# A two-block sequence model on one core: side sequences moved inside a merge of generators, two scheduling offsets exchanged, weight pieces cut in halves

## Chip, cores, metric

The kernel runs on one core of one Trainium2 chip, as one launch. The metric is the device time of that launch in microseconds; the median of several runs is compared.

## What is computed

Two blocks on 256 tokens of width 2048, in float32. The first block has two layers over a latent sequence x and a context of 256 tokens; the second block is a single layer with four mixers, cross attention and a gated feed-forward. The change touches layer 0 (`even_mixer`) and layer 1 (`odd_mixer`) of the first block:

```python
def wkv7_scan(state, inputs, reverse):
    def step(S, xs):
        r, w, k, v, a, b = xs
        sa = jnp.einsum('bhvk,bhk->bhv', S, a)
        S = S * w[:, :, None, :] + sa[..., None] * b[:, :, None, :] + v[..., None] * k[:, :, None, :]
        return S, jnp.einsum('bhvk,bhk->bhv', S, r)
...
def even_mixer(hl, hc, w_in, w_out, ...):
    al, rl, kl, vl, wdl, adl, gl = split_even(hl @ w_in)
    ac, rc, kc, vc, wdc, adc, gc = split_even(hc @ w_in)
    for d, reverse in enumerate((False, True)):
        in_c = rwkv_dir_inputs(rc, kc, vc, wdc[..., d, :], adc[..., d, :], *dir_p, reverse)
        in_l = rwkv_dir_inputs(rl, kl, vl, wdl[..., d, :], adl[..., d, :], *dir_p, reverse)
        s_ctx, y_c = wkv7_scan(s0, in_c, reverse)
        _, y_l = wkv7_scan(s_ctx, in_l, reverse)
        outs_l.append(rwkv_readout(y_l, in_l, r_k, gn_g[d], gn_b[d]))
...
def odd_mixer(hl, hc, w_in, w_out, q_g, k_g, cos, sin, need_ctx_out):
    ql, kl, vl, gl = jnp.split(hl @ w_in, ...)
    ol = blocked_attention(ql, k_all, v_all)
    yl = (ol.reshape(B, T, ATT_W) * jax.nn.silu(gl)) @ w_out
```

## The kernel before

**Numbers.** A float32 product of a large weight is made of fast passes: a weight piece is loaded as `raw`, cast to `whi` on ACT and its rest `raw - whi` put into `wlo` on DVE (`wsplit`, L187 and L188), and PE multiplies both halves. A piece is 128 partitions x 1024 columns in most of the kernel. `wsplit` cuts it into `s.nsplit` parts along its first free axis; `s.nsplit` is 1, and 2 inside `l0` (`small_stream`, L499 and L500, has pieces of 128x512 of its own there).

**Layer 0's recurrence.** It is done in chunks of 64 tokens. There are 16 units: 8 pairs of heads times 2 directions, 8 chunks each (4 of context, then 4 of x). A unit goes through generators, each of which emits some instructions per step and yields:

- `wkv_prep`, the preparation: shifts of r, k, v, two LoRA products (L625, L626), the decay scan (L638), the sum of squares of the keys (L641), the bonus (L671), the scaled keys BK (L680, L682). 14 steps.
- `wkv_inv`, the inverse: the stacked operand S (L704, L705) and BH (L710), then eight products per group of four chunks (L725), emptied by three DVE operations per half (L726, L730, L731), then the inverse of a triangular 64x64 block per chunk and head by products in the "iv" buffers (L741), each followed by DVE (L748 to L771). 20 steps.
- `wkv_rows`: transposes into "sc" buffers (L781, L789) and ACT copies out of them (L784, L786, L790), for four chunks at a time.
- `wkv_chain`, the serial part: per chunk the products L809, L815, L819 and the outputs L823, L824; between them R on DVE (L811), UV on ACT (L816) and the next state ZV on DVE (L822). 24 steps.
- `wkv_read`, the read-out: a mean (L841), a variance (L848, L849), an inverse root (L851) and the result (L853 to L856). 6 steps.

**The PSUM buffers.** There are eight banks: "acc", "sc" and "iv" have two buffers each, "ch" and "yb" one. Rows, the first products of the inverse, the preparation and the read-out all take "sc" in turn.

**The order.** `l0_body` runs a software pipeline: in turn n it merges the chain of unit n, the inverse of unit n+1, and, as side sequences, the read-out of unit n-1 and the preparation of unit n+2. `merge(a, b, side)` is a loop: in each pass it advances the inverse a by 3/4 of a step (by one, where there is no chain), the chain b by one, and each side sequence by one, and then emits `fill`, an even share of the dense products of layer 0 that are still open (L509 to L511) and of the modulation products (L369, L382, L392). A turn has some 26 passes. PE's order is exactly the order in which the code emits (`manual_schedule(engines={ET.PE})`). DVE, ACT, POOL and SP are ordered by a list scheduler at build time: among instructions that it takes to be ready, the one with the lowest number goes first; the number is the place in the program, less an offset given by `s.prio(n)`, which calls `high_priority(offset=n)`:

```python
    def prio(s, n):
        return s.tc.high_priority(offset=n) if n else contextlib.nullcontext()
```

On the chip every engine works through its own list in that order.

**Layer 1** (`l1`) gets its 140 weight pieces through `stream`, which splits a piece ahead of its use; layer 0's output projection (`l0_out_n`) is emitted in `l1` for three of its four column blocks, 24 more pieces.

Of the kernel before, what the change touches and what calls it, by code (L numbers as in the profile page):

```python
# [136 lines left out]
class _K:  # L137
# [729 lines left out]
    def l0_body(s):  # L867
# [60 lines left out]
        def fill(t):  # L928
            nonlocal F
            credit[0] += t  # L930
            while credit[0] > 0.0:
                c = next(F, None)
                if c is None:
                    return
                credit[0] -= c
                left[0] -= c
# [7 lines left out]
        def prep(n):  # L944
            p, d = units[n]
            if d == 0:
                while s.have_rkv < p:
                    fill(0.6)
                s.raw = s.l0_raw(p)
                s.outp = s.T("op", [P, 512], bufs=3)  # L950
            u = _U(p, d, s.raw, s.outp)
            u.h = [None, None]
            return u, s.wkv_prep(u)
# [2 lines left out]

        def merge(a, b, side):

            due = 0.25
            while a is not None or b is not None:  # L960
                due += 0.75 if b is not None else 1.0
                if a is not None and due >= 1.0:
                    due -= 1.0
                    with s.prio(100):
                        if next(a, None) is None:
                            a = None
                if b is not None:
                    with s.prio(60):
                        if next(b, s) is s:
                            b = None  # L970
                for x in side:
                    next(x, None)
                steps[0] = max(steps[0] - 1.0, 1.0)
                fill(left[0] / steps[0])
            for x in side:
                for _ in x:
                    pass

# [5 lines left out]
        cur, pg = prep(0)  # L984
# [12 lines left out]
        F = filler([r.rearrange("p (k c) -> p k c", k=2) for r in raw[0:2]])  # L997
        credit[0], left[0] = 0.0, 29 * 16 * 0.64 + 16 * (4 * 0.6 + 0.9)
        nxt, pg = prep(1)
        merge(s.wkv_inv(cur, 1), None, [pg])  # L1000
        s.wkv_rows(cur, 0)
        rg = []
        for n in range(16):
            s.wkv_rows(cur, 1)
            nx2, pg = prep(n + 2) if n < 14 else (None, iter(()))
            if n == 15:
                for _ in F:
                    pass
                s.out0 = F = s.l0_out_n(0)
                credit[0], left[0], steps[0] = 0.0, 26, 24.0  # L1010
            merge(s.wkv_inv(nxt, n % 2) if nxt else None, s.wkv_chain(cur, nxt, rg), rg + [pg])
            rg = [s.wkv_read(cur)]
            cur, nxt = nxt, nx2
        for _ in rg[0]:
# [1115 lines left out]
def build(tc, I, O, dbg=False, upto=99):  # L2130
    nc = tc.nc
    s = _K(tc, I, O, dbg)
    s.nraw = 4
    s.nhi = 2
    s.nsplit = 1
    s.ivn = [0, 0]
    s.psb = {"acc": 2, "sc": 2, "iv": 2, "ch": 1, "yb": 1}
    with tc.tile_pool(name="sb", bufs=1) as s.pool, tc.tile_pool(name="ps", bufs=1, space=PSUM) as s.psum, \
            tc.tile_pool(name="dr", bufs=1, space=DRAM) as s.dpool:
        ET = mybir.EngineType  # L2140
        head = s.head()
        with tc.manual_schedule(engines={ET.PE, ET.Activation}):
            next(head)
        with tc.manual_schedule(engines={ET.PE}):
            next(head, None)
            s.l0()
            s.mem_again()
            s.l1()
        s.block2()


# [16 lines left out]
```

## Time and profile before

| | |
|---|---|
| median of 3 runs | 3675.69 us (3669.39 to 3677.23) |
| the profiled execution | 3661.04 us |
| its span, first to last instruction | 3659.3 us |
| PE busy | 3455.7 us, 94% |
| weight loads of PE busy | 2701.6 us, 74% |
| DVE busy | 2189.3 us, 60% |
| ACT busy | 1637.9 us, 45% |
| mean granted clock of PE | 0.978 |

Busy time is the union of an engine's instructions over the span. The granted clock is a share of TensorE's full 2.4 GHz. A wait is idle time of an engine ahead of an instruction, put down to the instruction that released it last. The recurrence lies at about 590 to 1600 us, layer 1 at about 1790 to 2290 us.

### The profile page before, as it was taken

What the parts mean: (1) busy time and instruction counts of PE and PEld (TensorE: products, weight loads), DVE (VectorE), ACT (ScalarE), POOL (GpSimd) and SP (SyncE); (2) the same over time, 40 slices, a digit from 0 to 9 for tenths busy, and PEclk for the clock granted to TensorE, in tenths of its full rate; (3) what the DMA queues carried; (4) which work ended last, traced back from release to release, by engine and by line L of the source; (5) the groups of instructions that cost most, each with busy time, mean ns of one, the idle gap of its engine ahead of it and who ended that gap; (6) DMA issues with size and microseconds to landing.
All of it is one profiled execution on the core that took longest, in us unless ns stands there. A gap on an engine that the chain in (4) does not pass through costs nothing.

```text
span 3659.3 us, 56514 instructions
## 1 busy us (share of the span) xinstructions
PE 3455.7 (94%) x22385; PEld 2701.6 (74%) x22385; DVE 2189.3 (60%) x3813; ACT 1637.9 (45%) x2661; POOL 67.4 (2%) x136
## 2 busy tenths in 40 slices
PE   6999999989988888899999999998999999999998
PEld 3577775666666666678788888777888888888886
DVE  4254456667667666753656667766654566666544
ACT  3254224444454444431445555454454544444433
POOL 1000000000000000000000000000000000000000
PEclk9999999999999999999999999998999999999999
DMA  9974434433334333443434457553665566666654
GB/s 312 316 254 122 128 108 152 134 106 119 120 110 129 106 109 118 153 125 110 131 111 142 127 170 210 153 138 100 184 179 163 182 190 190 190 190 190 201 190 162
DMA packets 656579, 578.58 MB, mean 158 GB/s; under 512 B 25819, under 2 KB 499343, under 8 KB 656314
## 3 DMA queue, kind: packets, MB, share of 16 engines
q1 hardware_dynamic: 627936, 538.86, 49.0%
q10 hardware_dynamic: 24474, 29.09, 2.4%
q0 software_dynamic: 3904, 7.01, 0.7%
q8 instruction: 176, 2.88, 0.3%
q14 instruction: 89, 0.73, 0.1%
HBM read 547.32 MB, written 27.56 MB: 157 GB/s over the span
## 4 chain that ended last, share of the span: by engine, by line
issue 59%; PE 27%; DVE 5%; ACT 3%; DMA 2%; POOL 0%; ACTq 0%; SPq 0%; DVEq 0%; POOLq 0%
PE acc L509 4%; PE acc L510 4%; PE acc L511 4%; PE iv L741 3%; PE acc L369 2%; PE ch L815 1%; PE acc L207 1%; PE ch L819 1%; DMA sgT<-ev 1%; PE ch L809 1%; PE sc L725 1%; PE yb L823 1%; PE yb L824 0%; PE acc L1627 0%; PE acc L1628 0%
## 5 line engine op out<-in xcount | busy, mean ns | idle before, releaser
L188 DVE TENSOR_TENSOR wlo<-raw,whi 128x1024 fp32r<-128x1024 f32 (+2 forms) x742 | 850.9, 1150 | 850.6 <-ACT whi L187 845.5
L187 ACT CAST whi<-raw 128x1024 fp32r<-128x1024 f32 (+2 forms) x742 | 732.2, 990 | 1060.0 <-PE acc L207 209.7
L207 PE MATMUL acc<-A,whi 128*128 128x512 f32 x1488 | 530.1, 397 | 2.6 <-DVE A L1059 1.5
L208 PE MATMUL acc<-A,wlo 128*128 128x256 f32 x1488 | 423.3, 285 | 0.9 <-DVE wlo L188 0.9
L509 PE MATMUL acc<-A,whi 128*128 128x512 f32 x768 | 353.0, 460 | 18.5 <-ACT ev L520 12.4
L207 PEld LDWEIGHTS acc<-A,whi 128*128 128x128 f32 x1488 | 277.9, 187 | 66.8 <-DVE A L1059 1.8
L510 PE MATMUL acc<-B,whi 128*128 128x512 f32 x768 | 308.5, 402 | 0.0
L511 PE MATMUL acc<-A,wlo 128*128 128x512 f32 x768 | 306.8, 399 | 0.0
L208 PEld LDWEIGHTS acc<-A,wlo 128*128 128x128 f32 x1488 | 280.3, 188 | 5.3 <-DVE wlo L188 2.1
L207 PE MATMUL iv<-A,whi 128*128 128x512 f32 x736 | 257.4, 391 | 0.0
L509 PEld LDWEIGHTS acc<-A,whi 128*128 128x128 f32 x768 | 149.4, 195 | 84.7 <-issue 35.8
L208 PE MATMUL iv<-A,wlo 128*128 128x256 f32 x736 | 206.3, 280 | 2.5 <-DVE wlo L188 2.5
L511 PEld LDWEIGHTS acc<-A,wlo 128*128 128x128 f32 x768 | 148.2, 193 | 34.2
L510 PEld LDWEIGHTS acc<-B,whi 128*128 128x128 f32 x768 | 149.3, 194 | 29.9 <-issue 11.3
L207 PEld LDWEIGHTS iv<-A,whi 128*128 128x128 f32 x736 | 137.7, 187 | 30.3
L208 PEld LDWEIGHTS iv<-A,wlo 128*128 128x128 f32 x736 | 139.1, 189 | 3.1 <-DVE wlo L188 3.1
L500 DVE TENSOR_TENSOR wlo<-raw,whi 128x512 fp32r<-128x512 f32 x116 | 80.0, 689 | 70.1 <-ACT whi L499 69.1
L499 ACT CAST whi<-raw 128x512 fp32r<-128x512 f32 x116 | 71.6, 617 | 112.2 <-PE acc L510 105.3
L816 ACT COPY UV<-ch 64x128 f32<-64x128 f32 x128 | 32.9, 257 | 162.2 <-PE ch L815 152.7
L822 DVE SCALAR_TENSOR_TENSOR ZV<-ZV,We,ch 64x64 f32<-64x64 f32 x224 | 62.0, 277 | 35.4 <-PE ch L819 33.0
L224 PE MATMUL acc<-whi,B 128*128 128x512 f32 x192 | 76.7, 401 | 0.0
L225 PE MATMUL acc<-wlo,B 128*128 128x512 f32 x192 | 75.8, 395 | 0.2 <-DVE wlo L188 0.2
(1577 smaller groups left out, 7076.5 us busy)
## 6 DMA issues: line engine op xcount, KB each, us to landing
raw<-w_gate_up SPq DMA_DIRECT2D x176, 512.0 KB, 4.8
raw<-mod_w SPq DMA_DIRECT2D x128, 512.0 KB, 4.8
raw<-w_down SPq DMA_DIRECT2D x88, 512.0 KB, 4.8
raw<-od_w_in SPq DMA_DIRECT2D x80, 512.0 KB, 3.7
raw<-w_in SPq DMA_DIRECT2D x80, 512.0 KB, 3.9
raw<-w_xkv SPq DMA_DIRECT2D x64, 512.0 KB, 6.5
A<-mod_w SPq DMA_DIRECT2D x64, 512.0 KB, 5.8
raw<-ev_w_in SPq DMA_DIRECT2D x116, 256.0 KB, 3.0
```

The costliest lines, as they stand in the source:

```text
L187: nc.scalar.copy(hi[:, q], raw[:, q])
L188: nc.vector.tensor_sub(lo[:, q], raw[:, q], hi[:, q].bitcast(F32))
L207: s.nc.tensor.matmul(acc, hi, x.rearrange("p a t -> p (a t)"), start=start, stop=False)
L208: s.nc.tensor.matmul(acc[:, 0:256], lo, x[:, 0], start=False, stop=stop)
L224: nc.tensor.matmul(acc, xh, hi[:, kk], start=k == 0, stop=False)
L225: nc.tensor.matmul(acc, xh, lo[:, kk], start=False, stop=False)
L369: nc.tensor.matmul(acc[32 * q:32 * q + 32], s.SC[:, 2 * k:2 * k + 32], pair[q // 2][:, q % 2], start=k < 4, stop=k >= 12, tile_position=(0 ...
L500: nc.vector.tensor_sub(lo, raws[j % 2], hi.bitcast(F32))
L509: s.nc.tensor.matmul(acc, hi[:, k], hX[kx], start=kx == 0, stop=False)
L510: s.nc.tensor.matmul(acc, hi[:, k], lX[kx], start=False, stop=False)
L511: s.nc.tensor.matmul(acc, lo[:, k], hX[kx], start=False, stop=kx == 15)
L741: nc.tensor.matmul(ps[hs[h], c], l(hs[h], c), r(hs[h], c), start=True, stop=True)
```

## The change

In `merge` the inverse is emitted under offset 60 instead of 100 and the chain under 120 instead of 60. A side sequence now comes with the number of the pass from which it is advanced: the read-out from pass 3, the preparation from pass 7, or from pass 5 in the first merge, which has no chain. Before, both were advanced from pass 1. What is left of them at the end of a merge is emitted there, as before. And `l1` runs with `s.nsplit = 2`.

```diff
         def merge(a, b, side):
 
-            due = 0.25
+            due, n = 0.25, 0
             while a is not None or b is not None:
                 due += 0.75 if b is not None else 1.0
                 if a is not None and due >= 1.0:
                     due -= 1.0
-                    with s.prio(100):
+                    with s.prio(60):
                         if next(a, None) is None:
                             a = None
                 if b is not None:
-                    with s.prio(60):
+                    with s.prio(120):
                         if next(b, s) is s:
                             b = None
-                for x in side:
-                    next(x, None)
+                n += 1
+                for x, first in side:
+                    if n >= first:
+                        next(x, None)
                 steps[0] = max(steps[0] - 1.0, 1.0)
                 fill(left[0] / steps[0])
-            for x in side:
+            for x, _ in side:
                 for _ in x:
                     pass
...
-        merge(s.wkv_inv(cur, 1), None, [pg])
+        merge(s.wkv_inv(cur, 1), None, [(pg, 5)])
...
-            merge(s.wkv_inv(nxt, n % 2) if nxt else None, s.wkv_chain(cur, nxt, rg), rg + [pg])
+            merge(s.wkv_inv(nxt, n % 2) if nxt else None, s.wkv_chain(cur, nxt, rg), [(x, 3) for x in rg] + [(pg, 7)])
...
+            s.nsplit = 2
             s.l1()
+            s.nsplit = 1
```

The lines of the generators keep their numbers. The instructions of layer 0 are the same in number and kind on every engine. The list of PE in the opening of one unit, that of the timeline from 997 us, before; L725 are the inverse's products, L848 the read-out's second, L625 and L626 the preparation's LoRA products, L509 to L511 filler, the L8xx of "ch" and "yb" the chain:

```order
L725 MATMUL sc<-S_9494,BK 128x128 x8
L819 MATMUL ch<-UV_9075,BT_9077 128x128
L823 MATMUL yb<-whi,ZV_9076 128x128
L824 MATMUL yb<-pu,UV_9075 128x128
L848 MATMUL sc<-sq,k_65 128x512
L509 MATMUL acc<-A_1576,whi 128x512
L510 MATMUL acc<-B_1584,whi 128x512
L511 MATMUL acc<-A_1576,wlo 128x512
L725 MATMUL sc<-S_9501,BK 128x128 x8
L809 MATMUL ch<-ZV_9076,whi 128x128
L625 MATMUL sc<-TW,m_9531 128x512
L626 MATMUL sc<-TW,m_9531 128x512
```

The same place on PE now; the read-out's first product L841 stands where the second stood, and the second follows L815:

```order
L725 MATMUL sc<-S_9491,BK 128x128 x8
L819 MATMUL ch<-UV_9043,BT_9045 128x128
L823 MATMUL yb<-whi,ZV_9044 128x128
L824 MATMUL yb<-pu,UV_9043 128x128
L841 MATMUL sc<-YS,k_65 128x512
...
L725 MATMUL sc<-S_9498,BK 128x128 x8
L809 MATMUL ch<-ZV_9044,whi 128x128
L509 MATMUL acc<-A_1576,whi 128x512
L510 MATMUL acc<-B_1584,whi 128x512
L511 MATMUL acc<-A_1576,wlo 128x512
L815 MATMUL ch<-R_9578,pw 128x128
L848 MATMUL sc<-sq,k_65 128x512
```

The LoRA products have left the opening. The second place on PE is the middle of a unit, behind the rows of the next one (L781, L789); now L641, the preparation's sum of squares, stands there, as L841 stood behind the rows at a unit's start before:

```order
L781 MATMUL sc<-k_65,m_8831 128x128 x2
L789 MATMUL sc<-k_65,BH 128x128 x4
L809 MATMUL ch<-ZV_9461,wlo 128x128
L641 MATMUL sc<-tb,k_65 128x512
L509 MATMUL acc<-A_1574,whi 128x512
```

Before, L641 stood ahead of these rows, behind the fourth chunk's L809. DVE in the opening of that unit before, up to the chain's second R (L811) and one more; L726, L730 and L731 empty the inverse's products, L853 and L856 are the read-out's last:

```order
L731 TENSOR_TENSOR AB_9510<-sc,k_65 128x4x64
L822 SCALAR_TENSOR_TENSOR ZV_9076<-ZV_9076,We,ch 64x64 x2
L853 TENSOR_TENSOR YS<-YS,sq 128x512
L726 TENSOR_TENSOR raw<-sc,k_65 64x256
L730 TENSOR_TENSOR S_9501<-sc,k_65 64x4x64
L731 TENSOR_TENSOR AB_9513<-sc,k_65 128x4x64
L726 TENSOR_TENSOR raw<-sc,k_65 64x256
L730 TENSOR_TENSOR S_9501<-sc,k_65 64x4x64
L731 TENSOR_TENSOR AB_9513<-sc,k_65 128x4x64
L732 TENSOR_TENSOR raw<-raw,id_83 128x512
L811 TENSOR_TENSOR R_9605<-ch,k_65 128x128
L856 TENSOR_TENSOR op<-op,YS 128x512
```

And DVE there now:

```order
L726 TENSOR_TENSOR raw<-sc,k_65 64x256
L822 SCALAR_TENSOR_TENSOR ZV_9044<-ZV_9044,We,ch 64x64 x2
L731 TENSOR_TENSOR AB_9507<-sc,k_65 128x4x64
L730 TENSOR_TENSOR S_9491<-sc,k_65 64x4x64
L731 TENSOR_TENSOR AB_9507<-sc,k_65 128x4x64
L446 SCALAR_TENSOR_TENSOR vs<-v_9486,PM,tb 128x512
L842 SCALAR_TENSOR_TENSOR YS<-sc,YS 128x512
L726 TENSOR_TENSOR raw<-sc,k_65 64x256
L730 TENSOR_TENSOR S_9498<-sc,k_65 64x4x64
L731 TENSOR_TENSOR AB_9510<-sc,k_65 128x4x64
L811 TENSOR_TENSOR R_9578<-ch,k_65 128x128
L726 TENSOR_TENSOR raw<-sc,k_65 64x256
```

The chain's ZV (L822) and R (L811) moved in between the operations that empty the inverse's products, and L853 moved behind all of them.

## Rows read from the trace of the kernel before

**Rows 1.** Windows by stage: window and length, busy us per engine (instructions), PEclk, DMA, GB/s.

```profile
590.00:1600.00 1010.00, 891.76 (x9390) 636.67 (x9389) 685.93 (x1475) 465.19 (x899) 41.54 (x83) 0.95 0.39 120
...
1790.00:2290.00 500.00, 495.22 (x2383) 402.89 (x2382) 323.86 (x540) 266.77 (x408) 0.00 (x0) 1.00 0.52 154
```

**Rows 2.** Waits of PE, 590 to 1600 us: waiter, awaited, us, times, longest.

```profile
PE sc L625 <- DVE pv L731: 20.8, 14, 3.1
PE sc L625 <- DVE AB L731: 18.2, 12, 2.7
PE sc L841 <- ACT ZV L786: 17.5, 15, 1.4
PE ch L809 <- DVE ZV L822: 16.7, 14, 3.0
...
PE iv L741 <- DVE Y L753: 6.7, 11, 2.6
PE sc L725 <- ACT sq L849: 4.8, 4, 2.9
...
PE sc L848 <- DVE AB L731: 1.0, 2, 0.5
```

**Rows 3.** Waits of PE, 400 to 600 us, the first merge.

```profile
PE sc L625 <- DVE pv L731: 4.4, 1, 4.4
```

**Rows 4.** Timeline of PE in one opening: start, us, instruction, [idle before].

```profile
1001.34 0.47 PE L815 MATMUL ch<-R,pw 128*128 128x128 f32 x2
...
1002.34 0.39 PE L509 MATMUL acc<-A,whi 128*128 128x512 f32 x1
...
1007.19 1.95 PE L725 MATMUL sc<-S,BK 128*128 128x128 f32 x16
1008.98 0.39 PE L809 MATMUL ch<-ZV,whi 128*128 128x128 f32 x2
1011.53 0.47 PE L625 MATMUL sc<-TW,m 128*128 128x512 f32 x1 [2.16 <-DVE AB L731]
```

**Rows 5.** Timeline of DVE in the same opening.

```profile
1009.36 0.69 DVE L853 TENSOR_TENSOR YS<-YS,sq 128x512 f32<-128x512 f32 x1 [2.13 <-ACT sq L851]
1010.09 0.42 DVE L726 TENSOR_TENSOR raw<-sc,k 64x256 f32<-64x256 f32 x1
```

**Rows 6.** Windows around the end of that wait.

```profile
1009.00:1012.80 3.80, 1.07 (x6) 0.47 (x4) 3.31 (x8) 1.67 (x3) 0.00 (x0) 1.00 0.00 0
1013.20:1016.60 3.40, 3.40 (x11) 2.72 (x10) 2.83 (x6) 1.69 (x4) 0.31 (x1) 0.50 0.00 0
```

**Rows 7.** Windows of 23 us at the starts of units 1 and 13.

```profile
664.00:687.00 23.00, 17.77 (x114) 12.68 (x113) 14.96 (x36) 13.73 (x27) 0.31 (x1) 1.00 0.38 120
...
1483.00:1506.00 23.00, 19.45 (x130) 13.45 (x129) 14.44 (x34) 13.68 (x24) 1.61 (x3) 0.93 0.44 139
```

**Rows 8.** Groups by line and form: count, busy us, mean ns, idle before.

```profile
L188 DVE TENSOR_TENSOR wlo<-raw,whi 128x1024 fp32r<-128x1024 f32 x640 | 783.3, 1224 | 730.0 <-ACT whi L187 725.2 <-PE iv L369 1.9 <-PE ch L2059 1.2
...
L188 DVE TENSOR_TENSOR wlo<-raw,whi 128x512 fp32r<-128x512 f32 x100 | 66.7, 689 | 119.3 <-ACT whi L187 119.1
...
L187 ACT CAST whi<-raw 128x1024 fp32r<-128x1024 f32 x640 | 672.2, 1050 | 911.0 <-PE acc L207 206.4 <-issue 157.2 <-PE acc L226 110.0
...
L187 ACT CAST whi<-raw 128x512 fp32r<-128x512 f32 x100 | 59.3, 618 | 145.6 <-PE acc L510 92.0 <-issue 24.7 <-PE acc L202 7.9
```

**Rows 9.** Waits of PE in layer 1, 1790 to 2290 us.

```profile
PE acc L1236 <- DVE wlo L188: 1.8, 2, 1.5
...
PE acc L208 <- DVE wlo L188: 0.2, 1, 0.2
```

**Rows 10.** Lines L682 and L704: count, ns min/median/max, first and last start.

```profile
L682 DVE TENSOR_TENSOR BK<-kp,wi x16: 681/685/692, 355.6 to 1512.4; 128x512 f32<-128x512 f32 x16
...
L704 DVE TENSOR_TENSOR S<-kk,w x32: 406/420/425, 564.4 to 1546.4; 64x256 f32<-64x256 f32 x32
```

**Rows 11.** Windows behind the openings, 14 of them, their sum.

```profile
sum 622.00, PE 577.30 PEld 404.70 DVE 454.61 ACT 258.40 POOL 31.80; mean PE 41.24 PEld 28.91 DVE 32.47 ACT 18.46 POOL 2.27
```

## The prediction

> **What bounds the kernel now.** First the windows by stage [rows 1]; the columns to read are PE's busy time, DVE's and PEclk. From 590 to 1600 us, the loop over the 16 units (head pair, direction) of the recurrence, PE is busy 891.8 of 1010 us, so it idles 118.2 us, and its granted clock is 0.95. In layer 1 (1790 to 2290) it idles 4.8 of 500 us at full clock. PE is the bound in both; in the loop it is a bound with holes. DVE is busy 685.9 of the 1010 us: not full, and yet PE waits for it.
>
> Second, who ends the holes [rows 2]. PE issues its matmuls in the order written, so each wait has a place in the code. Three kinds belong to the "sc" tiles, two PSUM buffers that rows, read-out, inverse and preparation share. The preparation's LoRA product L625 waits 39.0 us in 26 waits (20.8 + 18.2) for L731, the last of the three DVE operations that empty a buffer of the inverse's first products. The read-out's L841 waits 17.5 us in 15 for L786, ACT's copies of the rows. The inverse's products L725 wait 4.8 us for the read-out's L849. Together that is 61.3 of the 118.2 us. In the first merge, ahead of the loop, L625 waits 4.4 us more [rows 3].
>
> Third, one opening of a unit as a timeline, on PE [rows 4] and on DVE [rows 5]. The second eight products of the inverse (16 records) start at 1007.19. DVE begins to empty them only at 1010.09, for L853 of the read-out stands ahead of L726 in its order and waited 2.13 us for ACT. PE was through L809 by 1009.4 and started L625 at 1011.53. Then the clock [rows 6]: behind a stretch of 3.8 us with 1.07 us of PE work the granted clock is 0.50, that is 1.2 GHz, for 3.4 us. Nearly every opening shows the same: of 13 windows of 23 us, at the starts of units 1 to 13, one has 1.00, nine 0.93 and three 0.85 [rows 7], so 23 x (9 x 0.07 + 3 x 0.15) = 24.8 us of PE time are lost there.
>
> **The change part by part.** It adds and removes no operation in layer 0: it moves the two side sequences and changes two scheduling offsets.
>
> *LoRA products of the preparation.* They go from merge step 4, right behind the inverse's second products, to step 10, with a read-out product and some five steps between; at 1010/16 = 63 us per unit and some 26 steps, a step is 2.4 us. The buffers have long been emptied by then: -39.0 - 4.4 = **-43.4 us**.
>
> *First product of the read-out.* L841 no longer follows the rows: **-17.5**. It now stands where L848 stood, behind eight L725, L819, L823 and L824. There L848 waited 1.0 us in two waits [rows 2], the lower end. The upper end is the mean of L625's waits, 39.0/26 = 1.5 us, in 14 units: 21. DVE's new order puts a chain operation inside the emptying of that buffer, so I take a value between, 0.5 us in each of 14: **+7**.
>
> *Second product of the read-out.* L848 now stands behind the second products, with L809, a filler group and L815 between. Lower end 0; upper end the first of the two LoRA waits that it replaces there, 20.8 us, 1.5 each. L815 and one group take 1.0 us (1001.34 to 1002.34 in [rows 4]), so 0.5 x 14: **+7**. L725's wait for L849 goes, since the buffer it needs is now emptied by DVE's L842: **-4.8**.
>
> *L641 of the preparation* now comes right behind the next unit's rows and one L809, in all 14 units: just where L841 was. It inherits that wait, 17.5/15 = 1.17 us each: **+16.4** (0 if ACT is free earlier, 17.5 at most).
>
> *The clock.* If the hole in the opening goes, the slow stretch behind it should go too. Between 0 and 24.8 us, I take two thirds: **-16**.
>
> *Offsets.* On DVE and ACT the chain (60, now 120) goes ahead of the inverse (100, now 60). L809 waits 16.7 us for the chain's L822, the inverse's L741 6.7 us for L753 [rows 2]. The first should shrink and the second grow, and the preparation's DVE work now falls among the later chain steps, where waits of the first kind can come back. From -16.7 to +16.7 I take **+4**. No DMA is added; on SP the loads of rkv pieces and weights change places by a few issues, which I cost at nothing, as none of the waits in [rows 2] is for a DMA.
>
> *Layer 1's halves.* 164 pieces (140 of layer 1, 24 of layer 0's output weights) are cast and subtracted as two of 128x512 instead of one of 128x1024: on DVE 2 x 689 - 1224 = 154 ns more, on ACT 2 x 618 - 1050 = 186 ns more [rows 8]. That is 25 and 31 us in all beside PE, on engines busy 323.9 and 266.8 of 500 us [rows 1]. What it can win is what PE waits for a piece there: 1.8 + 0.2 us [rows 9]. What it can lose: 34 groups of products end in an evacuation that stands behind at most one instruction more, 34 x 0.154 = 5.2 us. I take **0**, from -2.0 to +5.2. The Trainium skill, Perfetto Trace Analysis, section Optimizing Scalar/DVE Operations, says that breaking up instructions may finish work sooner where ACT and DVE are not full but cause bubbles on other engines; by it this half would win something, and the trace leaves it 2.0 us.
>
> Sum: -43.4 - 17.5 - 4.8 + 7 + 7 + 16.4 - 16 + 4 = **-47.3 us**. The profiled execution took 3661.0 us (span 3659.3), so 3613.7; the median of the runs, 3675.7, lies 14.7 above it, and by that measure the forecast is **3628 us**. With all terms at one end it would be 108 faster, at the other 16 slower.
>
> **Rivals.**
>
> *Slower: the preparation comes too late.* It now ends at step 21 instead of 14, and the next unit's first products, at its step 3, need its last DVE work: L680 and L682 (0.685 us each) and four of L704 and L705 (0.42 each) [rows 10], 3.05 us. If DVE is behind, PE waits for these in each of 14 units, 43 us, with a slow stretch as in [rows 6] behind it that costs half of 3.4 us, 24 us in all: +67 - 47 = +20, about 3695. It decides once DVE lags PE by more than the some eight steps between, 19 us. For it: behind the openings DVE is busy 454.6 of 622 us already [rows 11]. Against it: 19 us is much. Chance 0.10.
>
> *The bubble moves.* Two buffers and the same uses; what waited comes back at L841, L848 and L641, near 17.5, 20.8 and 16.4: -65.7 + 54.7 = -11, and no clock won: 3665. The Trainium skill, Perfetto Trace Analysis, section Optimization Strategy, says that a gap that repeats on the engine that should be full can mean too few SBUF or PSUM buffers; by it a new order of the same uses would end here. The trace shows the repeat, but also that L641 and L671, later in the unit, wait for none of these buffers now. Chance 0.14, of which 0.09 over 0.2% faster.
>
> *More than forecast.* All 24.8 us of clock, L841 and L848 at their lower ends (1 and 0), the chain's 16.7 us gone: -65.7 + 16.4 + 1 - 24.8 - 16.7 = -90: 3586. Chance 0.13.
>
> *Nothing moves.* PE's and DVE's orders differ in every unit, so only 0.03, with no change of the time.
>
> **How the numbers follow.** The forecast (3600 to 3655) has 0.60. Faster by over 0.2% (7 us, about what a measurement of this kernel can tell from no change): 0.60 + 0.13 + 0.09 = 0.82. Within: 0.05 + 0.03 = 0.08. Slower: 0.10. The range from 3586 to 3678 leaves out the slower rival and about half of the larger gain.
>
> **What would show it.** Right: L625 gone from PE's waits, L641 in them with about 16 us for L786, the loop shorter by some 45 us, the clock of the openings near 1. Wrong: L725 waiting for L682 or L705 at the openings (the preparation late); L841 and L848 waiting tens of us for L731 (the bubble moved); layer 1 longer by over 5 us.

## The result, and the profile after

The changed kernel takes 3611.60 us (median of 4 runs, 3609.00 to 3614.81) against 3672.54 us before, run beside it: a ratio of 0.9834, 95% interval 0.9817 to 0.9851, 61 us faster. The forecast was 3628 us, 47 us faster. The profiled execution took 3612.74 us with a span of 3610.9.

In the two traces, whose spans differ by 48.4 us, the stretch from the inverse's first product to the first product of layer 0's output projection is 57.5 us shorter; why the spans differ by less is taken up in the last section. First the window of the kernel before from 530.4 to 1591.7 us, then that of the changed one from 530.2 to 1534.0, which hold the same matmuls up to one record (columns as in [rows 1]):

```profile
530.40:1591.70 1061.30, 936.67 (x9920) 665.18 (x9919) 723.64 (x1542) 482.46 (x934) 41.99 (x84) 0.95 0.39 121
```

```profile
530.20:1534.00 1003.80, 900.77 (x9919) 646.27 (x9918) 718.99 (x1541) 476.75 (x928) 40.56 (x84) 0.98 0.41 128
```

PE's idle time falls from 1061.3 - 936.7 = 124.6 to 103.0 us, by 21.6. Its busy time falls by 35.9 us for the same instructions, while the granted clock rises from 0.95 to 0.98: more of the gain came through faster matmuls than through the waits themselves. Added up over windows of 10 us, the half clock (0.50) takes 106 us of this stretch before and 37 us now (55 us in the changed kernel's second trace, after_again). At half clock half of that time is lost, so 34 us came back, and that is nearly all of the 35.9.

Who is waited for now, in that window of the changed kernel (to compare with [rows 2]; up to L856 the lines have kept their numbers):

```profile
PE iv L741 <- DVE AT L748: 22.7, 14, 2.6
PE iv L741 <- DVE Y L753: 17.1, 24, 2.1
PE sc L641 <- ACT ZV L786: 17.0, 14, 2.1
...
PE ch L809 <- DVE ZV L822: 5.2, 7, 1.7
...
PE ch L815 <- DVE R L811: 4.9, 6, 2.8
...
PE sc L841 <- DVE AB L731: 2.9, 3, 1.1
```

L625 has left the list, in the first merge too [rows 3], and so have L848 and L725's wait for L849. L641 waits for the copies of the rows as L841 did, and L841 waits a little for L731. New at the top is L741 for L748, 22.7 us in 14 waits. The changed kernel's lists show where that comes from. First DVE, in an opening like that of [rows 5]:

```profile
993.15 0.43 DVE L749 TENSOR_TENSOR T<-inv,k 128x512 f16<-128x512 f16 x1 [0.44 <-ACT inv L734]
995.10 0.69 DVE L853 TENSOR_TENSOR YS<-YS,sq 128x512 f32<-128x512 f32 x1 [1.52 <-ACT sq L851]
995.70 0.69 DVE L500 TENSOR_TENSOR wlo<-raw,whi 128x512 fp32r<-128x512 f32 x1
996.42 0.69 DVE L748 TENSOR_TENSOR AT<-iv,k 128x512 f16<-128x512 f32 x1
```

Then PE at the same time:

```profile
990.15 1.02 PE L848 MATMUL sc<-sq,k 128*128 128x512 f32 x2
...
993.85 0.44 PE L741 MATMUL iv<-id,inv 64*64 64x64 f16 x16
...
997.16 0.44 PE L741 MATMUL iv<-AT,inv 64*64 64x64 f16 x16 [1.46 <-DVE AT L748]
```

And ACT, which L853 waited for:

```profile
990.63 1.28 ACT L849 ACT_TABLE_LOAD   x1
991.93 0.69 ACT L849 ACTIVATE sq<-sc,eps 128x512 f32<-128x512 f32 x1
...
993.14 1.28 ACT L851 ACT_TABLE_LOAD   x1
994.43 0.63 ACT L851 ACTIVATE sq<-sq 128x512 f32<-128x512 f32 x1
```

The read-out's second product ends at 991.2. ACT loads a table (1.28 us), takes the logarithm, loads a table again, takes the exponential and is done at 995.06. DVE has reached L853 by then and waited 1.52 us. L748, which empties the inverse's first round and whose input was there at 994.3, stands two places behind it and starts at 996.42. PE waits 1.46 us. In [rows 5] the same L853 stood ahead of L726. It is the same obstacle, moved.

The clock of the openings, of 13 windows of 23 us, the first and the last (to compare with [rows 7]):

```profile
670.50:693.50 23.00, 19.51 (x170) 14.10 (x168) 14.89 (x36) 11.90 (x23) 0.00 (x0) 1.00 0.39 129
...
1431.10:1454.10 23.00, 19.87 (x166) 15.09 (x165) 15.37 (x36) 10.27 (x20) 0.54 (x1) 0.93 0.39 124
```

Eleven of them are at 1.00 and two at 0.93: 3.2 us lost where 24.8 were before.

### The profile page after: what moved, and what is told of

It reads as the page before. It is cut to its first block, busy times and chain, and to the rows that moved or that the text cites. A ratio compares the mean times of both kernels' runs of the same rounds, so it can differ in the third digit from the quotient of the medians.

```text
span 3610.9 us, 56799 instructions
## 1 busy us (share of the span) xinstructions
PE 3433.2 (95%) x22385; PEld 2687.5 (74%) x22385; DVE 2197.2 (61%) x3977; ACT 1649.2 (46%) x2825; POOL 66.4 (2%) x136
## 4 chain that ended last, share of the span: by engine, by line
issue 59%; PE 5%; DVE 2%; ACT 1%; DMA 0%; POOL 0%; ACTq 0%; POOLq 0%; SPq 0%; DVEq 0%
PE iv L741 1%; PE acc L509 1%; PE acc L510 1%; PE acc L511 1%; PE sc L725 0%; PE acc L369 0%; PE ch L815 0%; DVE Y L753 0%; ACT L851 0%; ACT L849 0%; PE ch L819 0%; DMA raw<-catT 0%; PE ch L809 0%; PE sc L841 0%; PE yb L823 0%
## 5 line engine op out<-in xcount | busy, mean ns | idle before, releaser
L188 DVE TENSOR_TENSOR wlo<-raw,whi 128x1024 fp32r<-128x1024 f32 (+1 forms) x906 | 865.3, 969 | 838.0 <-ACT whi L187 832.2
L187 ACT CAST whi<-raw 128x1024 fp32r<-128x1024 f32 (+1 forms) x906 | 749.3, 844 | 1054.2 <-PE acc L207 203.1
L207 PE MATMUL acc<-A,whi 128*128 128x512 f32 x1488 | 535.4, 402 | 1.1 <-ACT whi L187 0.8
L509 PE MATMUL acc<-A,whi 128*128 128x512 f32 x768 | 348.7, 454 | 20.8 <-ACT ev L520 14.4
L207 PEld LDWEIGHTS acc<-A,whi 128*128 128x128 f32 x1488 | 278.8, 187 | 69.2 <-issue 1.6
L511 PE MATMUL acc<-A,wlo 128*128 128x512 f32 x768 | 302.3, 394 | 0.0
L207 PE MATMUL iv<-A,whi 128*128 128x512 f32 x736 | 262.3, 399 | 0.0
L509 PEld LDWEIGHTS acc<-A,whi 128*128 128x128 f32 x768 | 146.5, 191 | 83.8 <-issue 34.1
L511 PEld LDWEIGHTS acc<-A,wlo 128*128 128x128 f32 x768 | 145.3, 189 | 33.0
L510 PEld LDWEIGHTS acc<-B,whi 128*128 128x128 f32 x768 | 146.6, 191 | 29.1 <-issue 11.5
L207 PEld LDWEIGHTS iv<-A,whi 128*128 128x128 f32 x736 | 138.4, 188 | 34.1
L741 PEld LDWEIGHTS <-inv 64*64 64x64 f16 x1536 | 33.5, 110 | 66.2 <-issue 63.7
L741 PEld LDWEIGHTS <-T 64*64 64x64 f16 x1536 | 35.3, 110 | 55.4 <-issue 50.8
```

What stands on the lines that cost most here:

```text
L187: nc.scalar.copy(hi[:, q], raw[:, q])
L188: nc.vector.tensor_sub(lo[:, q], raw[:, q], hi[:, q].bitcast(F32))
L207: s.nc.tensor.matmul(acc, hi, x.rearrange("p a t -> p (a t)"), start=start, stop=False)
L509: s.nc.tensor.matmul(acc, hi[:, k], hX[kx], start=kx == 0, stop=False)
L510: s.nc.tensor.matmul(acc, hi[:, k], lX[kx], start=False, stop=False)
L511: s.nc.tensor.matmul(acc, lo[:, k], hX[kx], start=False, stop=kx == 15)
```

## The experiments

All were timed beside the kernel before, whose median was 3670.0 us in each of the rounds from e1_halves on and 3672.5 beside the changed kernel. The stage is the stretch from the inverse's first product to the output projection's first, read from one trace of each kernel; idle is its length less PE's busy time in it. Where the table gives the preparation a later start, it also starts from pass 5 in the first merge; in e5_prep1, too, only the loop's start is put back.

| kernel | read-out, preparation from pass | offsets | halves | stage us | PE idle in it | median us | ratio (95%) |
|---|---|---|---|---|---|---|---|
| before | 1, 1 | old | no | 1061.3 | 124.6 | 3672.5 | |
| changed | 3, 7 | new | yes | 1003.8 | 103.0 | 3611.6 | 0.9834 (0.9817 to 0.9851) |
| e1_halves | 1, 1 | old | yes | 1063.8 | 127.3 | 3664.5 | 0.9988 (0.9973 to 1.0003) |
| e2_offsets | 1, 1 | new | no | 1060.9 | 121.2 | 3660.3 | 0.9981 (0.9964 to 0.9997) |
| e3_starts | 3, 7 | old | no | 1016.0 | 112.4 | 3627.8 | 0.9891 (0.9870 to 0.9912) |
| e4_layer0 | 3, 7 | new | no | 1006.0 | 102.8 | 3606.0 | 0.9846 (0.9823 to 0.9870) |
| e5_prep1 | 3, 1 | new | yes | 1024.8 | 107.1 | 3620.4 | 0.9868 (0.9847 to 0.9889) |
| e6_read1 | 1, 7 | new | yes | 1026.0 | 110.9 | 3627.1 | 0.9887 (0.9869 to 0.9904) |
| e7_read2_late | 3 (second product later), 7 | new | yes | 987.4 | 87.1 | 3601.6 | 0.9812 (0.9796 to 0.9828) |
| e8_prep8 | 3, 8 | new | yes | 998.4 | 92.9 | 3599.9 | 0.9812 (0.9792 to 0.9832) |
| e9_both | 3 (second product later), 8 | new | yes | 981.4 | 79.1 | 3594.4 | 0.9784 (0.9761 to 0.9808) |
| after_again | 3, 7 | new | yes | 1006.5 | 99.9 | 3608.0 | 0.9831 (0.9808 to 0.9854) |

**Layer 1's halves alone.**

```diff
+            s.nsplit = 2
             s.l1()
+            s.nsplit = 1
```

> The kernel before with layer 1's pieces split in two halves, and nothing else. Theory (the gain of the change lies in the merge of layer 0): no difference, within 4 us of the kernel before; the stretch from layer 1's first product to its last stays at 489 us. Rival (the halves carry part of the 61 us): 8 us or more faster, with that stretch shorter.

3664.52 us, ratio 0.9988, an interval that holds 1. The first fence is of the kernel before, the second of e1_halves. They show one group of layer 1's products, which takes 210.8 us from its first to its last in the kernel before and 210.4 with the halves; over all products of that line it is 444.6 and 443.6 us:

```profile
L1235 PE MATMUL acc<-whi,A x128: 387/389/799, 1905.5 to 2116.3; 128*128 128x512 f32 x128
```

```profile
L1235 PE MATMUL acc<-whi,A x128: 387/389/799, 1910.2 to 2120.6; 128*128 128x512 f32 x128
```

The halves are worth nothing that can be seen, and e4_layer0, which lacks them, is as fast as the changed kernel.

**The offsets alone.**

```diff
-                    with s.prio(100):
+                    with s.prio(60):
                         if next(a, None) is None:
...
-                    with s.prio(60):
+                    with s.prio(120):
                         if next(b, s) is s:
```

> The kernel before with the chain's offset 120 and the inverse's 60, side sequences advanced from pass 1 as before, no halves. Theory (the places of the side sequences on PE decide): L625 still waits over 30 us for L731 and the openings still run partly at half clock; L809's wait for L822 falls from 16.7 to about 6 us; in all 0 to 15 us faster. Rival (the order on DVE decides, wherever the side sequences stand on PE): 30 us or more faster, L625's waits below 15 us.

3660.30 us, ratio 0.9981: 7 us by the ratio, with an interval that ends just short of 1, and the stage is as long as before, 1060.9 us, with a granted clock of 0.95 as before. L809's wait for L822 fell to 9.2 us (about 6 was expected), and L625 still waits 44.8:

```profile
PE sc L625 <- DVE pv L731: 25.5, 14, 3.6
PE sc L625 <- DVE AB L731: 19.3, 12, 3.1
...
PE ch L809 <- DVE ZV L822: 9.2, 9, 2.6
```

**The later starts alone.**

```diff
-        merge(s.wkv_inv(cur, 1), None, [pg])
+        merge(s.wkv_inv(cur, 1), None, [(pg, 5)])
...
-            merge(..., rg + [pg])
+            merge(..., [(x, 3) for x in rg] + [(pg, 7)])
```

> The kernel before with the later starts of the side sequences (3, 7, 5) and the old offsets (chain 60, inverse 100), no halves. Theory: L625 no longer waits, L641 waits about 17 us for L786, little half clock in the openings; 35 to 55 us faster. Rival (the offsets decide): 25 us faster or less.

3627.76 us, ratio 0.9891: 40 us faster, as the theory had it. But the stage is 10 to 12 us longer than with the new offsets, though the offsets alone shorten it by 0.4. The waits tell why:

```profile
PE ch L815 <- DVE R L811: 30.0, 21, 3.8
PE sc L641 <- ACT ZV L786: 16.9, 14, 1.9
...
PE iv L741 <- DVE AT L748: 9.8, 11, 2.5
```

L815 waits 30.0 us for the chain's R. One opening of e3_starts, on DVE and on PE:

```profile
993.58 0.28 DVE L811 TENSOR_TENSOR R<-ch,k 128x128 f32<-128x128 f32 x1
...
993.92 0.49 PE L815 MATMUL ch<-R,pw 128*128 128x128 f32 x2 [1.72 <-DVE R L811]
```

By the lists of the two engines, R (L811) stands on DVE behind all that empties the inverse's second products under the old offsets. In the kernel before, the LoRA products and a filler group stood on PE ahead of L815 and covered that; here only a filler group does. With the new offsets R stands in the middle of the emptying, and the wait is 4.9 us. In return L748 is waited for 9.8 us here and 22.7 in the changed kernel.

**Both, without the halves.**

Against the changed kernel:

```diff
-            s.nsplit = 2
             s.l1()
-            s.nsplit = 1
```

> The changed kernel without layer 1's halves: later starts and new offsets. Theory: 57 to 61 us faster than the kernel before, as the changed kernel is. Rival (the halves carry part): 50 us or less.

3605.98 us, ratio 0.9846, stage 1006.0 us: the changed kernel's gain without the halves.

**The preparation back in the opening.**

Against the changed kernel, as in all that follow:

```diff
-            merge(..., [(x, 3) for x in rg] + [(pg, 7)])
+            merge(..., [(x, 3) for x in rg] + [(pg, 1)])
```

> The changed kernel with the preparation from pass 1 again in the loop (the read-out stays at pass 3, the offsets stay new). Theory (the LoRA products behind the inverse's products make the hole, and the hole the slow clock): L625 waits 25 to 45 us for L731 again, L641 no longer waits for L786, half clock in the loop back from 31 to over 60 us; 20 to 45 us slower than the changed kernel, 3632 to 3657. Rival (the read-out's place made the hole): within 12 us of the changed kernel.

The theory missed here: 3620.44 us, 9 us slower than the changed kernel by the medians, which is the rival's figure, 12 by the ratios and 21 by the stage (18 against the changed kernel's second trace). L625 waits 19.4 us, 14.7 of them for L731, and not 25 to 45:

```profile
PE sc L625 <- DVE AB L731: 11.3, 13, 4.2
...
PE sc L625 <- ACT ss L627: 4.7, 6, 0.8
...
PE sc L625 <- DVE pv L731: 3.4, 8, 0.8
```

The difference to e2_offsets, where it waits 44.8 (3.6 of them in the first merge), lies in the read-out, which no longer stands ahead of the products' emptying on DVE. Much of the LoRA products' wait went with the read-out's place. L748's wait falls to 6.1 us. PE's idle time is only 4.1 us longer than in the changed kernel's first trace and 7.2 longer than in its second; its busy time is longer by 17.0 and by 11.1. So most of the loss is clock: the half clock takes 65 us of the stage, against 37 and 55, and over 60 was expected.

**The read-out back in the opening.**

```diff
-            merge(..., [(x, 3) for x in rg] + [(pg, 7)])
+            merge(..., [(x, 1) for x in rg] + [(pg, 7)])
```

> The changed kernel with the read-out from pass 1 again (the preparation stays at pass 7). Theory (L748 waits because the read-out's L853 stands ahead of it on DVE): L748's wait falls from 22.8 us to under 8, L841 waits about 17 us for the rows' L786 again, L853 is ahead of the second products' emptying; within 12 us of the changed kernel. Rival (the later read-out is worth its 17.5 us in full, and L748's wait is the inverse's own): L748 stays above 15 us, 15 to 25 us slower.

```profile
PE ch L815 <- DVE R L811: 21.8, 16, 2.4
PE sc L841 <- ACT ZV L786: 17.5, 15, 1.4
PE sc L641 <- ACT ZV L786: 16.2, 14, 1.6
...
PE iv L741 <- DVE AT L748: 2.6, 5, 1.0
```

L748's wait falls to 2.6 us, as the theory said, and yet the kernel is 15 us slower than the changed one (3627.08), 22 by the stage: the figure of the rival, which had expected L748's wait to stay. L841 waits 17.5 us again, and 21.8 us of waits for R take the place of L748's. On this kernel's DVE list L853 is back ahead of the emptying of the second products, and R behind it; that this makes R late is read from the list and was not tried by itself.

With e2_offsets, e5_prep1 and the changed kernel this makes a square with the offsets new throughout: from a stage of 1060.9 us, the read-out's later start alone takes 36.1 us, the preparation's alone 34.9, both together 57.1. (Each of the three also holds the 3.6 us that L625 waited in the first merge.) Either of them removes part of the same hole.

**The read-out's second product later.** From here on the trace of the changed kernel is acted on.

```diff
         nc.scalar.activation(sq, YS, AF.Square)
-        for _ in range(2):
+        for _ in range(5):
             yield
```

> The changed kernel with three more passes between the read-out's first and second product, so that L853 stands behind the chain's third L822 on DVE and no longer ahead of L748. Theory: L741's wait for L748 falls from 22.8 us to under 8 and the kernel is 10 to 20 us faster than the changed one, 3592 to 3602. Rival (the wait moves on to the next operation of DVE): the same within 6 us, with L753 or L811 waited for by 12 us more.

3601.59 us, ratio 0.9812, stage 987.4 us, 16.4 less than in the changed kernel's first trace and 19.1 less than in its second. The median is 10 us lower, but the intervals of the two ratios overlap. L748's wait is all but gone:

```profile
PE sc L641 <- ACT ZV L786: 22.9, 14, 4.0
...
PE iv L741 <- DVE Y L753: 12.5, 23, 1.5
PE ch L809 <- DVE ZV L822: 10.5, 7, 2.9
PE ch L815 <- DVE R L811: 4.4, 6, 2.3
...
PE iv L741 <- DVE AT L748: 1.8, 3, 1.0
```

So L853's place ahead of L748 did cost time, some 16 us of the 22.7 that were waited; the rest reappears, as L641's wait rose from 17.0 to 22.9 us and L809's from 5.2 to 10.5, while L753's fell. DVE itself still idles 26.4 us ahead of L853 in this kernel, against 29.0 in the changed one: what went is not that wait, but what stood behind it. PE's busy time, 900.3 us, is 0.5 us below that of the changed kernel's first trace and 6.4 below that of its second, so little slow clock hung on this hole.

**The preparation one pass later.**

```diff
-            merge(..., [(x, 3) for x in rg] + [(pg, 7)])
+            merge(..., [(x, 3) for x in rg] + [(pg, 8)])
```

> The changed kernel with the preparation from pass 8, so that L641 stands behind a filler group and L815 as well. Theory: L641's wait for L786 falls from 17 us to under 6, and the kernel is 6 to 14 us faster than the changed one, 3598 to 3606. Rival (the preparation becomes too late, or the wait moves on to L671 or the products): the same within 5 us, or slower, with waits of L725 for L682 or L705.

```profile
PE iv L741 <- DVE AT L748: 22.6, 14, 2.6
PE iv L741 <- DVE Y L753: 19.8, 19, 2.4
...
PE ch L815 <- DVE R L811: 8.9, 11, 2.9
...
PE sc L641 <- ACT ZV L786: 2.9, 4, 0.9
```

L641's wait falls from 17.0 to 2.9 us. The stage is 5.4 us shorter than in the changed kernel's first trace and 8.1 shorter than in its second, and waits for L753 and R rose by 6.7 together. The median, 3599.87, would allow 12 us, but its interval overlaps with the changed kernel's. How much of the 14 us of wait was won is settled only to between 5 and 12.

**Both of these.**

```diff
-        for _ in range(2):
+        for _ in range(5):
...
-            merge(..., [(x, 3) for x in rg] + [(pg, 7)])
+            merge(..., [(x, 3) for x in rg] + [(pg, 8)])
```

> The changed kernel with both: the read-out's second product three passes later, and the preparation from pass 8. Theory (the two waits are separate holes in the same turn): L748's wait stays under 4 us, L641's falls from 22.9 to under 6, and from the first product of the inverse to the first of the output projection the time is 10 us or more below the 987 us of the late second product alone; in all 15 to 30 us faster than the changed kernel, 3582 to 3597. Rival (PE meets the next wait of DVE, so that a hole closed is a hole moved): that stretch within 5 us of 987, with L753, L811 or L809 waited for by 10 us more.

```profile
PE iv L741 <- DVE Y L753: 14.8, 14, 2.4
PE ch L815 <- DVE R L811: 11.5, 19, 1.9
PE ch L809 <- DVE ZV L822: 10.4, 9, 2.9
...
PE iv L741 <- DVE AT L748: 2.1, 3, 1.1
PE sc L641 <- ACT ZV L786: 1.9, 4, 0.6
```

3594.35 us, ratio 0.9784, stage 981.4 us: the fastest kernel of all, 17 us below the changed one's median and 14 below that of its second timing beside it (after_again). Between theory and rival: against e7_read2_late L641's wait fell by 21 us to 1.9, and the stage by 6.0. PE's idle time fell by 8.0 us, so 13 of the 21 us came back elsewhere; 9.4 of these are waits for the next operations of DVE, R (11.5 us instead of 4.4) and L753 (14.8 instead of 12.5).

**The changed kernel once more**, with no edit.

> The changed kernel once more, beside it on the same chip. The stretch from the first product of the inverse to the first of the output projection should be within 4 us of the 1003.8 us of its first trace, whatever the later stages do; the feed-forward part has either of the two paces seen so far, 230 or 236 ns for the longer product.

3607.97 us, ratio 0.9831; stage 1006.5 us, 2.7 from the first trace. The feed-forward part ran at the same pace as in the first, the slower of the two that the last section shows.

## Why the prediction was right, and where it was not

The time, the direction and the main mechanism were right: the gain lies in the loop of layer 0, and the holes at the openings and the slow clock behind them are what went. By its own steps:

- **LoRA products, -43.4.** Their wait is gone. But the sum took it as theirs, and e5_prep1 shows 19.4 us of it left when only the read-out is moved. Since the change moves both, the term held.
- **First product of the read-out, -17.5 + 7.** The old wait is gone, the new one is 2.9 us: the row for L848 in that place, at the lower end, was the better guide.
- **Second product, +7, and L725, -4.8.** Neither waits now. The +7 was 7 too much.
- **L641, +16.4.** 17.0 us measured. The wait that one operation had in a place was inherited by the next one put there.
- **Offsets, +4.** Here a step failed. L809's wait fell by 11.5 us and L753's rose by 10.4, about what was said; but L748's 22.7 us were not foreseen. The text looked at the chain and at the preparation's DVE work. DVE's new order was known to have L853 behind the emptying of the products, and nobody asked what would be late next behind it. The term should have been near +22. The offsets alone do not make this wait: it is 9.8 us with the later starts under the old offsets (e3_starts), 6.1 with the preparation put back (e5_prep1) and 2.6 with the read-out put back (e6_read1), and only the three together give 22.7. In sum idle fell by 21.6 us, and the sum's own terms for it make 31.3.
- **The clock, -16.** Mis-sized the other way: busy time fell by 35.9 us. In the openings 21.6 us came back where the upper end was 24.8, and slow stretches elsewhere in the stage, which the term left out, gave some 13 more (the 34 us of the first section less these; by the second trace busy time fell by 30.0 in all). This error, 19.9 us, and the 9.7 us by which idle time fell short pull opposite ways and leave 10; that the sum came as near as it did is in part luck.
- **Halves, 0.** Right. The Trainium skill, Perfetto Trace Analysis, section Optimizing Scalar/DVE Operations, says that breaking up instructions may let work be completed sooner where ACT and DVE cause bubbles on other engines. The trace before had 2.0 us of such waits here, and e1_halves shows no gain (0.9988, an interval that holds 1).

Of the rivals, the late preparation did not happen: no L725 waits for L682 or L705. (Its count was one off: 14 steps from pass 7 end at pass 20, not 21, which leaves one step more of room.) The moved bubble was half true: against 65.7 us of waits that went, 19.9 came back at the two buffers (17.0 for L641, 2.9 for L841) and 22.7 at L748, which is no wait for a buffer. The Trainium skill, Perfetto Trace Analysis, section Optimization Strategy, says that a gap that keeps repeating on the engine that should be full can mean too little SBUF or PSUM for the next tile. Here the order alone, with the same two buffers, took two thirds of the waits away; whether a third buffer would have done so too was not tried.

## What to carry to other kernels

Where an engine works through a list in order, a wait belongs to the operation that stands ahead, not to the one that is named: look on the engine waited for, one or two places up, for a side operation that waits on a third engine. Two sequences that collide in one place should be moved apart together with the order of the engine that serves both; with the new offsets either of them took some 35 us off the stage here, and both took 57. Both under the old offsets took 45, and the offsets alone nothing. And a hole on PE can cost as much again in the clock behind it (here 21.6 us of idle time went, and 35.9 us of busy time for the same matmuls), so the price of a wait is not only its length. Not every hole has that price: in e7_read2_late 13 to 16 us of idle time went, and only 0.5 to 6.4 of busy time.

## What was not expected of the hardware

The feed-forward part of the second block, which no kernel here touches, ran at one of two paces, with the same instructions. In 200 us of it, at full clock, the changed kernel issued 1133 matmuls, e4_layer0 1156:

```profile
2950.00:3150.00 200.00, 200.00 (x1133) 173.58 (x1132) 132.72 (x194) 94.42 (x142) 0.00 (x0) 1.00 0.65 187
```

```profile
2950.00:3150.00 200.00, 200.00 (x1156) 176.34 (x1155) 135.56 (x199) 96.50 (x144) 0.00 (x0) 1.00 0.67 190
```

That is 2.0%. The mean of L207 there is 391 ns at the quicker pace (the kernel before, e1_halves, e4_layer0, e8_prep8; e9_both, which issued 1156 as well, shows 394) and 399 ns at the slower one (the changed kernel in both its traces, e2_offsets, e3_starts, e5_prep1, e6_read1, e7_read2_late). It accounts for some 10 us between the profiled executions of the kernel before and the changed one, which differ by 48.4 us of span though the stage differs by 57.5; what sets the pace was not found. No single edit sorts the two lists: kernels with and without the halves, and with and without the later starts, stand in both. No kernel was traced at both paces. The timed runs of one kernel spread as far (e9_both: 3580.04 to 3598.87), which would fit a pace that changes from execution to execution; the two traces of the changed kernel, both slow, do not show it. Differences under 10 us were therefore read from the stage and not from the total.

The granted clock of two executions of the same kernel differs as well: 0.98 in the stage of the changed kernel's first trace and 0.97 in its second, with busy times of 900.8 and 906.7 us, idle times of 103.0 and 99.9, and lengths only 2.7 us apart.
